# A two-layer decoder trunk on one core: other buffers, ties and positions for the loads and modulation rows of the second MLP product, and its last four steps bank by bank

## The chip, the cores and the metric

The kernel runs on 1 core of one Trainium2 chip. The metric is device time in microseconds (us) for one execution of the whole program. The engines are PE (TensorE, matrix products), DVE (VectorE), ACT (ScalarE), POOL (GpSimd) and SP (SyncE, which here only issues transfers). Each engine works through its own list of instructions in order; semaphores hold an instruction back until what it needs is there.

## What is computed

A trunk of two layers over x of 1024 tokens by 1024 channels, all in float32. Layer 0 has an S5 mixer, layer 1 a Mamba-2 mixer, and behind each mixer stands the same MLP:

```
def _sq_relu_mlp(h, w1, w2):
    a = jax.nn.relu(h @ w1)
    return (a * a) @ w2
...
    for i in range(DEPTH):                                   # DEPTH = 2
        mod = cond @ ada_w[i] + ada_b[i]
        sh1, sc1, g1, sh2, sc2, g2 = jnp.split(mod[:, None, :], N_MOD, axis=-1)
        h = _modulate(_rmsnorm(x, norm_mix_g[i]), sh1, sc1)
...
        x = x + g1 * y
        h = _modulate(_rmsnorm(x, norm_mlp_g[i]), sh2, sc2)
        x = x + g2 * _sq_relu_mlp(h, mlp_w1[i], mlp_w2[i])
    return _rmsnorm(x, final_norm_g)
```

The hidden width is 4096. `mod` is a row vector worked out from the condition c; `ada_w` is 1024 by 6144 for each layer.

## The kernel before

A float32 product is made of three matmuls: both factors are split into a high and a low part (`split`, L82 to L85: ACT makes the high part with a CAST, DVE subtracts it for the low part), and `mm3` (L113) issues high by high, high by low and low by high (L117, L118, L119).

Each MLP has two halves. `Up` (L462) makes the hidden activations in 16 pairs (`pair`, L541); it works in the PSUM banks named px and pv, reads its weights through the ring of four buffers `K.raw` (tile name raw), and writes the panels that the second half needs to DRAM. `mlp_down` (L583) makes the second product. Both use a scheme with 7 block products in place of 8. In `mlp_down` the products are q = 0 to 6, each of 8 steps s, 56 steps in all. A step has 24 matmuls of 128 by 128 by 512: two panels, four banks, three matmuls each.

A step goes through three stages. `load(n + 3)` issues its transfers three steps ahead on SP: for q = 0 the weights into two "held" tiles of 256 KB each (`raw_w`, L603), which stay for the products 1 to 3, for q > 0 the weights into `K.raw` (L608), and in each step the panel of 512 KB (`raw_b`, L613 to L615, tile name br) into one of four buffers. `prepare(n + 2)` splits the weights into whi and wlo and the panel into four tiles h01h, h01l to h71h, h71l. These are four steps deep: h01 and h11 serve the steps s = 0 and 4, h21 and h31 the steps 1 and 5, h41 and h51 the steps 2 and 6, h61 and h71 the steps 3 and 7. Then come the matmuls, and behind the last step of a product `evacuate` (L665) adds the four banks to x on DVE.

The held tiles are the other half of the same store: h00h to h70h hold the weights of the steps 0 to 3 of the first product (two each), h00l to h70l those of the steps 4 to 7.

Three other kinds of work are woven into the steps. The x tiles come back from DRAM on POOL, each behind a small ACT copy that ties the transfer to the step (L696). In layer 0, `extra()` does one of 48 modulation rows of the next layer: a transfer of 512 KB (L332) into one of two buffers and a DVE product of 1.22 us (L333). And `norm_steps` (L200) makes the norm that follows, one token half while q = 5 and 6 run, the other at the end: squares (L209), their sums over the tiles (L210), eight short matmuls (L215), an inverse square root in a dozen short DVE instructions (L217, L137 to L143), its spread over the partitions (L156).

A scheduler sets the final order on each engine out of the order in which the code asks, so an instruction can stand well ahead of where its step is written. In layer 0 the second product runs from 781 to 1104 us of the profiled execution, in layer 1 from 2195 to 2513 us.

Of the kernel before, what the change touches and what calls it, by code (L numbers as in the profile page):

```python
# [11 lines left out]
F32 = mybir.dt.float32  # L12
# [7 lines left out]
P = 128  # L20
# [3 lines left out]
KT = D // P  # L24
# [32 lines left out]
def blk(i, n=P):  # L57
    return slice(i * n, i * n + n)
# [19 lines left out]
def tmp(K, name):  # L78
    return K.tmp.tile([P, 512], F32, tag="t", bufs=6, name=name)
# [33 lines left out]
def mm3(K, ps, terms, start=True, stop=True, more=False):  # L113

    n = len(terms)
    for i, (wh, wl, xh, xl) in enumerate(terms):
        K.nc.tensor.matmul(ps, wh, xh, start=start and i == 0, stop=False, skip_group_check=more)  # L117
        K.nc.tensor.matmul(ps, wh, xl, start=False, stop=False, skip_group_check=more)  # L118
        K.nc.tensor.matmul(ps, wl, xh, start=False, stop=stop and i == n - 1, skip_group_check=more)  # L119
# [11 lines left out]
def rsqrt(K, y, v):  # L131

    V = K.nc.vector
    n = v.shape[1]
    i = K.tmp.tile([P, n], I32, tag="rsi", name="rsi")
    t = K.tmp.tile([P, n], F32, tag="rst", name="rst")
    V.tensor_scalar(i, v.bitcast(I32), 1, None, op0=ALU.logical_shift_right)  # L137
    V.tensor_scalar(i, i, -1, 0x5F3759DF, op0=ALU.mult, op1=ALU.add)
    yy = i.bitcast(F32)
    for _ in range(3):  # L140
        V.scalar_tensor_tensor(t, yy, -0.5, yy, op0=ALU.mult, op1=ALU.mult)
        V.tensor_tensor(t, t, v, op=ALU.mult)
        V.scalar_tensor_tensor(y, t, 1.5, yy, op0=ALU.add, op1=ALU.mult)  # L143
        yy = y
# [55 lines left out]
def norm_steps(K, x, half, each, bank, order):  # L200

    nc = K.nc
    ss = K.br.tile([P, HT], F32, tag="ss", name="ss", bufs=1)
    for n, k in enumerate(order):
        if n == 0:
            nc.scalar.activation(ss, x[k][half], AF.Square)
        else:
            sq = tmp(K, "sq")
            nc.scalar.activation(sq, x[k][half], AF.Square)  # L209
            nc.vector.tensor_tensor(ss, ss, sq, op=ALU.add)  # L210
        yield
    yield
    pt = bank(K)
    for j in range(4):
        nc.tensor.matmul(pt[:, j:j + 1], ss[:, blk(j)], K.ones, start=True, stop=True)  # L215
    v = K.tmp.tile([P, 4], F32, tag="rsv", name="rsv")
    nc.vector.tensor_scalar(v, pt[:, 0:4], 1.0 / D, EPS, op0=ALU.mult, op1=ALU.add)  # L217
    y = K.tmp.tile([P, 4], F32, tag="rsy", name="rsy")
    rsqrt(K, y, v)
    for _ in range(4):  # L220
        yield
    pb = spread(K, y, bank)
    for k in range(KT):
        each(k, pb)
        yield

# [50 lines left out]
def drain(gen):  # L277
    for _ in gen:
        pass
# [182 lines left out]
class Up:  # L462
# [9 lines left out]
    def bank(self, m):  # L472
        K = self.K
        return (K.ps if m % 4 < 2 else K.psb).tile([P, 512], F32, tag="ps", name="px")
# [108 lines left out]
def mlp_down(K, pool, x, bscr, w2, gate, xscr, mid, extra):  # L583

    nc, V = K.nc, K.nc.vector
    held = [h_tile(K, p % 8, 0, p // 8, F32) for p in range(16)]
    A11, A12, A21, A22 = range(4)

    def block(s, a, i):

        return w2[s, i, :, a * 256:a * 256 + 256].rearrange("i p c -> p i c")

    def raw_w(q, s):
        if q == 0:  # L600
            for j in range(2):
                d = held[2 * s + j].rearrange("p (i c) -> p i c", i=2)
                nc.sync.dma_start(d, block(s, A11, slice(2 * j, 2 * j + 2)))  # L603
            return None
        raws = []
        for a in ((A21,), (A22,), (A12,), (A21, A22), (A22,), (A12,))[q - 1]:
            t = K.raw.tile([P, 1024], F32, tag="raw", name="raw")
            nc.sync.dma_start(t.rearrange("p (i c) -> p i c", i=4), block(s, a, slice(0, 4)))  # L608
            raws.append(t)
        return raws  # L610

    def raw_b(q, s):
        t = (K.wz, pool)[s // 2 % 2].tile([P, 1024], F32, tag="br", name="br", bufs=2)  # L613
        t = t.rearrange("p (a t) -> p a t", a=2)
        nc.sync.dma_start(t, bscr[q][s].rearrange("a p t -> p a t"))  # L615
        return t

    def split_w(q, s, raw):
        wt = K.wring[(K.wturn + 1) % len(K.wring)]
        hd = held[2 * s:2 * s + 2]  # L620
        if q == 4:
            V.tensor_tensor(raw[0], raw[0], raw[1], op=ALU.add)  # L622
        if q > 2:
            return unit_of(K, raw[0])
        K.wturn = (K.wturn + 1) % len(K.wring)
        hi = wt.tile([P, 1024], F32R, tag="whi", name="whi")
        lo = wt.tile([P, 1024], F32R, tag="wlo", name="wlo")
        for j in range(2):
            c = half_of(j)
            if q == 1:  # L630
                V.tensor_tensor(hd[j], hd[j], raw[0][:, c], op=ALU.subtract)
            elif q == 2:
                V.tensor_tensor(hd[j], raw[0][:, c], hd[j], op=ALU.subtract)
            split(K, hi[:, c], lo[:, c], hd[j])
        return hi, lo

    def split_w3(s, raw):
        for j in range(2):
            c = half_of(j)
            V.tensor_tensor(raw[:, c], raw[:, c], held[2 * s + j], op=ALU.subtract)  # L640

    def split_b(s, t):
        b = []
        for j in range(2):
            k = (2 * s + j) % 8
            b.append((h_tile(K, k, 1, 0), h_tile(K, k, 1, 1)))
            split(K, *b[j], t[:, j])
        return b

    steps = [(q, s) for q in range(7) for s in range(8)]  # L650
    raws, ready = {}, {}

    def load(n):
        if n < len(steps):
            raws[n] = raw_w(*steps[n]), raw_b(*steps[n])

    def prepare(n):
        if n < len(steps):
            q, s = steps[n]
            w, b = raws.pop(n)  # L660
            if q == 3:
                split_w3(s, w[0])
            ready[n] = split_w(q, s, w), split_b(s, b)

    def evacuate(q, i, p):  # L665
        def add(m, f):
            V.scalar_tensor_tensor(x[m][f], p, gate[:, m:m + 1], x[m][f], op0=ALU.mult, op1=ALU.add)  # L667

        a, b = 2 * i, 2 * i + 1
        for m, f in (  # L670
            ((a, 1),), ((b, 0), (b, 1)), ((b, 1),), ((a, 0),), ((b, 0), (a, 0)), ((b, 1),), ((a, 1),)
        )[q]:
            add(m, f)

    def banks(q):
        if q in (0, 6):
            return [(K.ps if i < 2 else K.psb).tile([P, HT], F32, tag="ps", name="py") for i in range(4)]
        if q in (1, 3, 5):
            return [psw(K) if i < 3 else pss(K) for i in range(4)]

    for n in range(3):
        load(n)
    prepare(0)
    prepare(1)
    norms = iter(())
    X = None
    back = [(k, 1) for k in range(0, KT, 2)] + [(k, f) for k in range(1, KT, 2) for f in range(2)]
    back += [(k, 0) for k in range(0, KT, 2)]
    for n, (q, s) in enumerate(steps):
        load(n + 3)  # L690
        prepare(n + 2)
        (wh, wl), b = ready.pop(n)
        if 0 < n <= len(back):

            k, f = back[n - 1]
            nc.scalar.copy(x[k][f][:, 0:1], b[0][0][:, 0:1].bitcast(F32))  # L696
            nc.gpsimd.dma_start(x[k][f], xscr[k, :, half_of(f)])
        if s == 0:
            X = X if q == 4 or q == 2 else banks(q)
            if q == 0:  # L700
                first = X
            if q in (2, 4):
                X = first
        for j in range(2):
            for i in range(4):
                c = blk(2 * i + j)
                mm3(
                    K, X[i], [(wh[:, c], wl[:, c], *b[j])],
                    q not in (2, 4) and s == 0 and j == 0, s == 7 and j == 1, more=True,
                )  # L710
        if s == 7:
            for i in range(4):
                evacuate(q, i, X[i])
        if q == 4 and s == 7:
            norms = mid(0, lambda K: K.ps.tile([P, 512], F32, tag="ps", name="pn"), range(KT))
        elif q == 5 or q == 6 and s < 3:
            next(norms, None)
            next(norms, None)
        elif q == 6:
            if s == 3:  # L720
                drain(norms)
                norms = mid(1, pss, [1, 3, 5, 7, 0, 2, 4, 6])
            if s < 7:
                next(norms)
        extra()
    drain(norms)


# [1053 lines left out]
```

## Time and profile before

| | |
|---|---|
| median of 3 runs | 2531.93 us (2530.64 to 2536.54) |
| profiled execution, its own time | 2533.94 us |
| its span, first to last instruction | 2532.2 us |
| PE busy | 2451.7 us (97%) |
| DVE busy | 1914.6 us (76%) |
| ACT busy | 1167.9 us (46%) |
| mean granted clock of TensorE | 0.986 of full speed |

The span is 1.74 us shorter than the execution's own time. PE is busy nearly always, so that what can be won lies in the few places where it waits, and in what its clock does behind them: the granted clock has two levels, 2.4 GHz (1.00 in the rows) and 1.2 GHz (0.50), and a stretch with a value between has parts at either.

### The profile page before, as it was taken

The numbers are of one execution on the slowest core, as the hardware profiler recorded it, in microseconds if no ns is written. First come the engines' busy times: TensorE is split into PE (matmuls) and PEld (weight loads), VectorE is DVE, ScalarE is ACT, GpSimd is POOL, SyncE is SP. The second block draws the span as 40 slices with busy tenths as digits, with TensorE's granted clock in tenths as the row PEclk, the third lists the DMA queues.
The fourth block names the chain that finished last, engine by engine and source line by source line (L and its number), as shares of the span: only waits on it lengthen the run. The fifth ranks groups of instructions, "written<-read, shape, count | busy, mean of one in ns | idle before, by whom it ended". The sixth has DMA issues, their size and how long they took to land.

```text
span 2532.2 us, 32780 instructions
## 1 busy us (share of the span) xinstructions
PE 2451.7 (97%) x11624; PEld 1965.7 (78%) x11624; DVE 1914.6 (76%) x3265; ACT 1167.9 (46%) x1955; POOL 213.7 (8%) x400
## 2 busy tenths in 40 slices
PE   7999999999998999999999999999999999899997
PEld 2788788877776888777888878778888777688886
DVE  8798754967887997958596868789687777776664
ACT  4587412744444433534564655544255444444342
POOL 0010000112221000100000000000011222200000
PEclk9999999999999999999999999999999999999998
DMA  6576772467769979723455554584245666874752
GB/s 243 155 169 169 242 242 96 153 204 250 258 227 343 342 260 308 272 85 115 154 160 160 161 173 139 169 259 136 88 141 192 225 231 232 294 250 136 254 194 77
DMA packets 284645, 503.80 MB, mean 199 GB/s; under 512 B 22081, under 2 KB 162369, under 8 KB 284481
## 3 DMA queue, kind: packets, MB, share of 16 engines
q1 hardware_dynamic: 242496, 386.34, 47.3%
q0 software_dynamic: 32384, 106.98, 12.4%
q10 hardware_dynamic: 9600, 8.39, 1.0%
q8 instruction: 91, 1.49, 0.2%
q14 instruction: 74, 0.60, 0.1%
HBM read 364.27 MB, written 133.17 MB: 196 GB/s over the span
## 4 chain that ended last, share of the span: by engine, by line
PE 74%; issue 8%; DVE 6%; DMA 6%; ACT 4%; POOL 2%; SPq 0%; DVEq 0%; POOLq 0%; ACTq 0%
PE pd L118 10%; PE pd L117 10%; PE pd L119 10%; PE py L117 4%; PE py L118 4%; PE py L119 4%; PE px L117 3%; PE pm L117 2%; PE pm L118 2%; PE pm L119 2%; PE px L119 2%; PE px L118 2%; PE pv L117 2%; PE pv L118 2%; PE pv L119 2%
## 5 line engine op out<-in xcount | busy, mean ns | idle before, releaser
L84 ACT CAST whi<-raw 128x1024 fp32r<-128x1024 f32 x241 | 251.0, 1048 | 365.5 <-PE pd L118 146.3
L85 DVE TENSOR_TENSOR wlo<-raw,whi 128x1024 fp32r<-128x1024 f32 x241 | 293.2, 1218 | 113.6 <-ACT whi L84 110.2
L333 DVE SCALAR_TENSOR_TENSOR ada<-ada,cond 128x1024 f32<-128x1024 f32 x88 | 107.3, 1222 | 57.8 <-DMA ada<-in_ada 57.7
L498 ACT ACTIVATE s<-s 128x512 f32<-128x512 f32 x84 | 53.0, 631 | 158.5 <-DVE s L496 155.9
L390 POOL DMA_DIRECT2D hscr<-x x32 | 17.3, 541 | 953.6 <-DVE x L736 751.1
L1235 DVE SCALAR_TENSOR_TENSOR cacc<-cr,conv,cacc 128x1024 f32<-128x1024 f32 x72 | 91.7, 1279 | 0.9 <-ACT cacc L1216 0.8
L1288 ACT ACTIVATE L<-csb,cs 128x128 f32<-128x128 f32 x224 | 69.9, 391 | 38.4 <-DMA csb<-csr 33.7
L505 POOL DMA_DIRECT2D b<-s x96 | 51.8, 540 | 330.9 <-ACT s L499 281.7
L496 DVE TENSOR_TENSOR s<-s,px 128x512 f32<-128x512 f32 x60 | 41.0, 684 | 34.9 <-PE px L119 34.9
L496 DVE TENSOR_TENSOR s<-s,pv 128x512 f32<-128x512 f32 x36 | 24.7, 686 | 55.5 <-PE pv L119 55.5
L505 POOL DMA_DIRECT2D b<-tt x96 | 51.8, 540 | 43.0 <-DVE tt L510 25.8
L499 ACT ACTIVATE s<-s 128x512 f32<-128x512 f32 x84 | 53.2, 633 | 2.7
L1239 ACT ACTIVATE cth<-cacc 128x512 f32<-128x512 f32 x48 | 27.7, 625 | 41.4 <-DVE cacc L1235 41.3
L667 DVE SCALAR_TENSOR_TENSOR x<-py,mod,x 128x512 f32<-128x512 f32 x40 | 27.3, 744 | 25.6 <-PE py L119 25.6
L1215 ACT COPY cr<-pd 128x512 f32<-128x512 f32 x48 | 27.8, 579 | 35.0 <-PE pd L119 35.0
L1308 DVE SCALAR_TENSOR_TENSOR y<-xs,cst,pm 128x128 f32<-128x128 f32 x128 | 38.3, 342 | 4.8 <-PE pm L1305 4.8
L117 PE MATMUL pd<-h00h,whi 128*128 128x512 f32 (+1 forms) x97 | 39.7, 411 | 2.0 <-ACT h00h L237 1.8
L1106 ACT ACTIVATE gt<-pd,bgh 128x512 f32<-128x512 f32 x16 | 11.0, 685 | 65.5 <-PE pd L119 65.5
L117 PE MATMUL pd<-h01h,whi 128*128 128x512 f32 x97 | 39.4, 407 | 0.5 <-DVE h61h L736 0.5
L119 PE MATMUL pd<-h10h,wlo 128*128 128x512 f32 (+1 forms) x97 | 39.3, 405 | 0.0
L622 DVE TENSOR_TENSOR raw<-raw 128x1024 f32<-128x1024 f32 x16 | 19.6, 1225 | 26.0 <-DMA raw<-in_w 26.0
L118 PE MATMUL pd<-h00l,whi 128*128 128x512 f32 (+1 forms) x97 | 38.8, 400 | 0.4 <-DVE h00l L238 0.4
(996 smaller groups left out, 8173.0 us busy)
## 6 DMA issues: line engine op xcount, KB each, us to landing
raw<-in_w SPq DMA_DIRECT2D x204, 512.0 KB, 4.6
br<-b SPq DMA_DIRECT2D x112, 512.0 KB, 4.7
ada<-in_ada SPq DMA_DIRECT2D x96, 512.0 KB, 5.0
b<-s POOLq DMA_DIRECT2D x96, 256.0 KB, 2.9
b<-tt POOLq DMA_DIRECT2D x96, 256.0 KB, 3.8
csb<-csr SPq DMA_DIRECT2D x32, 512.0 KB, 4.5
raw<-in_w_xbc SPq DMA_DIRECT2D x24, 512.0 KB, 4.5
xscr<-cacc SPq DMA_DIRECT2D x24, 512.0 KB, 2.7
```

What stands on the lines that cost most here:

```text
L84: K.nc.scalar.copy(hi, src)
L85: K.nc.vector.tensor_tensor(lo, src, hi.bitcast(F32), op=ALU.subtract)
L117: K.nc.tensor.matmul(ps, wh, xh, start=start and i == 0, stop=False, skip_group_check=more)
L118: K.nc.tensor.matmul(ps, wh, xl, start=False, stop=False, skip_group_check=more)
L119: K.nc.tensor.matmul(ps, wl, xh, start=False, stop=stop and i == n - 1, skip_group_check=more)
L333: K.nc.vector.scalar_tensor_tensor(r, r, 1.0, K.cond, op0=ALU.mult, op1=ALU.mult, accum_out=acc)
L496: nc.vector.tensor_tensor(t, t, p, op=ALU.add)
L498: nc.scalar.activation(t, t, AF.Relu)
L499: nc.scalar.activation(t, t, AF.Square)
L505: self.K.nc.gpsimd.dma_start(self.bscr[DOWN.index(nm)][m // 2][m % 2], t)
L1235: V.scalar_tensor_tensor(acc, cr[:, t:t + L], K.cw[:, i, t:t + 1], acc, op0=ALU.mult, op1=ALU.add)
L1288: nc.scalar.activation(Lm[:, r, :], cb[:, r, :], AF.Relu, bias=S.cs[:, c0 + r:c0 + r + 1], scale=-1.0)
```

## The change

Four things are changed, all in `mlp_down` and in the generator `norm_steps`.

1. The panels of the first product (q = 0) go through the ring `K.raw` in place of the four br buffers.
2. `load` gets a token, a column of the step's own first panel tile. For q = 0 and s of 3 or more, an ACT copy of that one column into the held tile (128x1) stands ahead of the held tile's transfer, which so waits for the step: ten copies for each layer. `load` also comes behind `ready.pop`.
3. The modulation rows: two for each step in q = 0, one in q = 1 to 3, none in q = 4 and 5, one in the steps 0 to 3 of q = 6, the rest behind them. `norm_steps` yields once more, and the tiles of its last loop follow `order`.
4. The last four steps of q = 6 are taken bank by bank: all four steps of one bank (24 matmuls), its evacuation, a step of the last norm, then the next bank. This holds for both layers.

```diff
     pb = spread(K, y, bank)
-    for k in range(KT):
+    yield
+    for k in order:
         each(k, pb)
...
-    def raw_w(q, s):
+    def raw_w(q, s, after):
         if q == 0:
             for j in range(2):
+                if after is not None:
+                    nc.scalar.copy(held[2 * s + j][:, 0:1], after)
                 d = held[2 * s + j].rearrange("p (i c) -> p i c", i=2)
                 nc.sync.dma_start(d, block(s, A11, slice(2 * j, 2 * j + 2)))
...
     def raw_b(q, s):
-        t = (K.wz, pool)[s // 2 % 2].tile([P, 1024], F32, tag="br", name="br", bufs=2)
+        if q == 0:
+            t = K.raw.tile([P, 1024], F32, tag="raw", name="br")
+        else:
+            t = (K.wz, pool)[s // 2 % 2].tile([P, 1024], F32, tag="br", name="br", bufs=2)
...
-    def load(n):
+    def load(n, after=None):
         if n < len(steps):
-            raws[n] = raw_w(*steps[n]), raw_b(*steps[n])
+            raws[n] = raw_w(*steps[n], after), raw_b(*steps[n])
...
     for n, (q, s) in enumerate(steps):
-        load(n + 3)
+        if q == 6 and s == 4:
+            break
+        (wh, wl), b = ready.pop(n)
+
+        token = b[0][0][:, 0:1].bitcast(F32)
+        load(n + 3, token)
         prepare(n + 2)
-        (wh, wl), b = ready.pop(n)
...
-        elif q == 5 or q == 6 and s < 3:
+        elif q == 5 or q == 6:
             next(norms, None)
             next(norms, None)
...
-        extra()
+        if q == 0:
+            extra()
+        if q not in (4, 5):
+            extra()
+
+    drain(norms)
+    norms = mid(1, pss, [1, 3, 5, 7, 0, 2, 4, 6])
+    load(n + 3)
+    prepare(n + 2)
+    prepare(n + 3)
+    for i in range(4):
+        next(norms)
+    last = [ready.pop(n + s) for s in range(4)]
+    for i in range(4):
+        for s, ((wh, wl), b) in enumerate(last):
+            for j in range(2):
+                c = blk(2 * i + j)
+                mm3(K, X[i], [(wh[:, c], wl[:, c], *b[j])], False, s == 3 and j == 1, more=True)
+        evacuate(6, i, X[i])
+        next(norms)
     drain(norms)
```

What this does to the order of the instructions shows at three places.

SP, where the second product of layer 0 begins, before the change. b_84 to b_91 are the panels of the steps 0 to 7 of q = 0, b_92 and up those of q = 1; raw is a weight of q = 1, ada a modulation row. The sixteen held tiles and the panel b_84 stand ahead of these rows:

```order
L603 DMA h60l<-in_w 128x2x256
L603 DMA h70l<-in_w 128x2x256
L608 DMA raw<-in_w 128x4x256
L615 DMA br<-b_85 128x2x512
L615 DMA br<-b_88 128x2x512
L608 DMA raw<-in_w 128x4x256 x3
L615 DMA br<-b_89 128x2x512
L615 DMA br<-b_92 128x2x512
L615 DMA br<-b_86 128x2x512
L615 DMA br<-b_87 128x2x512
L332 DMA ada<-in_ada 128x1024 x2
L615 DMA br<-b_90 128x2x512
```

The same place with the change, from its beginning:

```order
L621 DMA br<-b_84 128x2x512
L621 DMA br<-b_85 128x2x512
L621 DMA br<-b_86 128x2x512
L621 DMA br<-b_87 128x2x512
L621 DMA br<-b_92 128x2x512
L606 DMA h00h<-in_w 128x2x256
L606 DMA h10h<-in_w 128x2x256
L606 DMA h20h<-in_w 128x2x256
L606 DMA h30h<-in_w 128x2x256
L606 DMA h40h<-in_w 128x2x256
L606 DMA h50h<-in_w 128x2x256
L606 DMA h60h<-in_w 128x2x256
```

The panels of the steps 2 and 3 (b_86, b_87) stand ahead of all held tiles, where before they stood behind them, four raws and five other panels; h00l, which stood ahead of h00h, now stands behind h70h, and the raws of q = 1, four of which stood ahead of b_84, behind all panels of q = 0.

ACT, same layer, behind the cast of the last held tile of step 2, before the change. x copies tie the return of x, s and r are of `Up`:

```order
L487 COPY s_6455<-px 128x512
L487 COPY s_6470<-pv 128x512
L84 CAST h01h<-br 128x512
L84 CAST h11h<-br 128x512
L84 CAST whi<-h00l 128x512
L84 CAST whi<-h10l 128x512
L84 CAST h21h<-br 128x512
L84 CAST h31h<-br 128x512
L573 ACTIVATE r<-px 128x512
L84 CAST whi<-h60h 128x512
```

With the change, from the cast of h21h on (ahead of it stand the same two copies, the casts of h01h and h11h, and the ties of h60h and h70h):

```order
L84 CAST h21h<-br 128x512
L604 COPY h00l<-h21h 128x1
L84 CAST h31h<-br 128x512
L604 COPY h10l<-h21h 128x1
L705 COPY x_6537<-h21h 128x1
L84 CAST whi<-h00l 128x512
L84 CAST h41h<-br 128x512
L84 CAST whi<-h10l 128x512
L84 CAST h51h<-br 128x512
L84 CAST h61h<-br 128x512
L574 ACTIVATE r<-px 128x512
L84 CAST whi<-h60h 128x512
```

The casts of the steps 2 and 3 (h41h, h51h, h61h) have moved up, ahead of r, and r now stands behind the casts of h00l and h10l, whose transfers are tied to h21h a few rows above.

DVE at the end of the kernel, before the change (the four evacuations, the four sums of squares, the start of the inverse square root):

```order
L667 SCALAR_TENSOR_TENSOR x_18804<-py,mod,x_18804 128x512
L667 SCALAR_TENSOR_TENSOR x_18808<-py,mod,x_18808 128x512
L667 SCALAR_TENSOR_TENSOR x_18812<-py,mod,x_18812 128x512
L667 SCALAR_TENSOR_TENSOR x_18816<-py,mod,x_18816 128x512
L210 TENSOR_TENSOR ss<-ss,sq 128x512 x4
L217 TENSOR_SCALAR rsv<-pn 128x4
```

With the change:

```order
L673 SCALAR_TENSOR_TENSOR x_18814<-py,mod,x_18814 128x512
L210 TENSOR_TENSOR ss<-ss,sq 128x512
L673 SCALAR_TENSOR_TENSOR x_18818<-py,mod,x_18818 128x512
L210 TENSOR_TENSOR ss<-ss,sq 128x512
L673 SCALAR_TENSOR_TENSOR x_18822<-py,mod,x_18822 128x512
L210 TENSOR_TENSOR ss<-ss,sq 128x512
L673 SCALAR_TENSOR_TENSOR x_18826<-py,mod,x_18826 128x512
L210 TENSOR_TENSOR ss<-ss,sq 128x512
L217 TENSOR_SCALAR rsv<-pn 128x4
```

Each sum now follows its own evacuation, so that one sum stands behind the last evacuation where four stood.

The modulation rows on DVE in layer 0, counted up to the split of a step's panel, before and with the change: 6 and 6 at step 8, 9 and 13 at step 11, 15 and 18 at step 14, 16 and 19 at step 15, 20 and 23 at step 18, 34 and 36 at step 31. Between the steps 36 and 42 (q = 4, s = 4 to q = 5, s = 2) stand 8 rows before and 3 with the change; the last four stand at the same place in both, right ahead of the inverse square root of the first norm half.

## Rows read from the trace of the kernel before

**Rows 1.** Waits of PE over the whole kernel: total us, times, longest us

```profile
PE py L117 <- ACT h41h L84: 10.7, 2, 5.9
PE px L117 <- ACT s L487: 6.1, 2, 3.1
```

**Rows 2.** 20-us stretches: PE, PEld, DVE, ACT, POOL busy (instructions), granted clock, DMA share, GB/s

```profile
760.00:780.00 20.00, 16.98 (x67) 13.47 (x66) 14.79 (x25) 8.03 (x14) 1.80 (x4) 0.91 0.97 328
780.00:800.00 20.00, 15.19 (x61) 11.88 (x60) 15.73 (x27) 9.76 (x22) 5.96 (x11) 0.91 1.03 373
800.00:820.00 20.00, 20.00 (x82) 16.26 (x81) 16.86 (x29) 7.67 (x16) 1.64 (x3) 0.92 0.90 323
820.00:840.00 20.00, 20.00 (x89) 16.49 (x89) 19.38 (x34) 9.36 (x20) 2.18 (x4) 1.00 0.99 348
1040.00:1060.00 20.00, 17.00 (x72) 13.74 (x71) 17.35 (x36) 8.04 (x12) 1.03 (x2) 0.91 0.78 264
...
2200.00:2220.00 20.00, 14.07 (x54) 10.91 (x53) 11.15 (x19) 6.99 (x15) 2.19 (x4) 0.83 1.01 355
```

**Rows 3.** ACT's timeline, second product's start: start, length, instruction, [idle before, releaser]

```profile
770.57 0.58 ACT L487 COPY s<-px 128x512 f32<-128x512 f32 x1
...
781.35 0.60 ACT L573 ACTIVATE r<-px 128x512 f32<-128x512 f32 x1 [0.61 <-PE px L119]
...
796.50 0.62 ACT L84 CAST h41h<-br 128x512 fp32r<-128x512 f32 x1 [0.23 <-DMA br<-b]
```

**Rows 4.** SP's timeline, same place: issues (the x4 are b_89, b_92, b_86, b_87)

```profile
775.02 3.96 SPq L615 DMA_DIRECT2D br<-b  x2
783.61 6.66 SPq L615 DMA_DIRECT2D br<-b  x4
```

**Rows 5.** PE's timeline, the fourth bank's first matmul in step 0, layer 0

```profile
783.25 0.39 PE L117 MATMUL py<-h01h,whi 128*128 128x512 f32 x1
```

**Rows 6.** DVE's and PE's timeline around the first norm half, layer 0

```profile
1009.62 1.23 DVE L333 SCALAR_TENSOR_TENSOR ada<-ada,cond 128x1024 f32<-128x1024 f32 x1 [3.03 <-DMA ada<-in_ada]
1041.63 1.22 DVE L333 SCALAR_TENSOR_TENSOR ada<-ada,cond 128x1024 f32<-128x1024 f32 x1 [1.46 <-DMA ada<-in_ada]
1047.16 0.15 DVE L217 TENSOR_SCALAR rsv<-pn 128x4 f32<-128x4 f32 x1
...
1051.53 1.35 PE L156 MATMUL pn<-ident,rsy 128*128 128x128 f32 x8 [3.00 <-DVE rsy L143]
```

**Rows 7.** The end of the kernel, DVE, ACT and PE

```profile
2510.97 2.84 DVE L667 SCALAR_TENSOR_TENSOR x<-py,mod,x 128x512 f32<-128x512 f32 x4 [18.61 <-PE py L119]
2511.81 2.66 ACT L209 ACTIVATE sq<-x 128x512 f32<-128x512 f32 x4 [20.18 <-DVE x L667]
2513.72 3.07 DVE L210 TENSOR_TENSOR ss<-ss,sq 128x512 f32<-128x512 f32 x4
2516.85 1.87 PE L215 MATMUL pn<-ones,ss 128*128 128x1 f32 x8 [3.83 <-DVE ss L210]
```

**Rows 8.** Panel splits on DVE and the matmuls that need them, steps 12 and 44

```profile
838.19 0.68 DVE L85 TENSOR_TENSOR h01l<-br,h01h 128x512 fp32r<-128x512 f32 x1
...
855.07 0.39 PE L117 MATMUL pm<-h01h,whi 128*128 128x512 f32 x1
...
1027.77 0.69 DVE L85 TENSOR_TENSOR h01l<-br,h01h 128x512 fp32r<-128x512 f32 x1
...
1030.88 0.40 PE L117 MATMUL pm<-h01h,whi 128*128 128x512 f32 x1
```

**Rows 9.** Modulation rows on DVE: the first, the 16th and the 19th of 48

```profile
800.55 1.22 DVE L333 SCALAR_TENSOR_TENSOR ada<-ada,cond 128x1024 f32<-128x1024 f32 x1
...
853.33 1.22 DVE L333 SCALAR_TENSOR_TENSOR ada<-ada,cond 128x1024 f32<-128x1024 f32 x1 [0.92 <-DMA ada<-in_ada]
...
865.64 1.23 DVE L333 SCALAR_TENSOR_TENSOR ada<-ada,cond 128x1024 f32<-128x1024 f32 x1 [0.48 <-DMA ada<-in_ada]
```

**Rows 10.** Everything on tile ada, 780 to 880 us: its last line

```profile
DMA to landing us min/median/max: 4.3/5.8/8.7
```

More of the change, by code (lines that the diff above doesn't have):

```diff
@@ L689, in mlp_down @@
     for n, (q, s) in enumerate(steps):
-        load(n + 3)
+        if q == 6 and s == 4:
[3 more added lines that the diff above has]
+        load(n + 3, token)
         prepare(n + 2)
-        (wh, wl), b = ready.pop(n)
         if 0 < n <= len(back):
             k, f = back[n - 1]
-            nc.scalar.copy(x[k][f][:, 0:1], b[0][0][:, 0:1].bitcast(F32))
+            nc.scalar.copy(x[k][f][:, 0:1], token)
             nc.gpsimd.dma_start(x[k][f], xscr[k, :, half_of(f)])
@@ L715, in mlp_down @@
             norms = mid(0, lambda K: K.ps.tile([P, 512], F32, tag="ps", name="pn"), range(KT))
-        elif q == 5 or q == 6 and s < 3:
+        elif q == 5 or q == 6:
             next(norms, None)
             next(norms, None)
[L719 to L724, printed above, removed]
-        extra()
+        if q == 0:
[17 more added lines that the diff above has]
+        next(norms)
     drain(norms)
```

## The prediction

> **What bounds the kernel now.** I read the waits of PE over the whole kernel first. PE is busy 97% of the span, so only its waits and the halved clock behind them are to be won. Two entries come once in each layer and lie where the change works: PE waits for the cast of h41h (10.7 us, 2 times) and for a copy of s (6.1 us, 2 times) [rows 1].
>
> The 20-us stretches price these waits, clock included: at full clock PE does 89 matmuls in a stretch, 0.2247 us each. Layer 0 has 61 and 82 in the two stretches behind the h41h wait, 28 and 7 short; layer 1 has 54, 35 short in one. So this wait costs 35 x 0.2247 = 7.9 us in each layer, more than its length because the granted clock of these stretches falls to 0.91 and 0.83. The stretch of the s copy has 67, 22 short: 4.9 us [rows 2]. The one in layer 1 waits as long [rows 1].
>
> ACT's timeline and SP's issues then give the cause. h41h belongs to step 2. Its cast runs at 796.50 and had waited for its panel [rows 3]; that panel (b_86) is the third of four panels that SP issued from 783.61 to 790.3, behind two earlier panels [rows 4]. The transfers ahead of it ran at 0.97 and 1.03 of the 16 DMA engines [rows 2]. So the panel of step 2 comes late by its place in SP's list. The s copy stands at 770.57 on ACT [rows 3], in order behind six casts of held tiles.
>
> A third wait is in layer 0 alone: the spread of the first norm half stands 3.00 us for the inverse square root, whose first instruction, rsv at 1047.16, comes behind modulation rows that waited for their transfers [rows 6]. That stretch has 72 matmuls; 8 of them are the short ones of the spread, 25 slots minus 0.7 us of their own is 4.9 us [rows 2]. At the end of the kernel the four sums take 3.07 us behind the last evacuation, and PE stands 3.83 us [rows 7].
>
> **The change part by part.**
>
> *Panels of q = 0 through the ring, and held tiles tied.* Now b_84 to b_87 take the four ring buffers that the first raws of q = 1 had, and are issued where those were, ahead of all held tiles. The cover for the casts of the steps 0 to 3 is then Up's own last pairs. What could be late next is a held tile of step 3 or later. Its tie is the cast of a panel three steps ahead of its use, 3 x 5.5 = 16.5 us (the steps 12 to 44 take (1030.88 - 855.07) / 32 = 5.5 us each [rows 8]), against at most 8.7 us from issue to landing in the rows that I have [rows 10], and about 2.5 us of casts and subtractions. That fits. So the h41h waits go: **-15.7 us** for both layers.
>
> *One transfer fewer ahead of the s copy.* h00l stood ahead of h00h on SP; now it stands behind. 256 KB (0.262 MB) at the stretch's 328 GB/s is 0.8 us [rows 2]. The casts ahead of the s copy are the same. The bounds are 0 and the whole 4.9 us for each layer; I take one transfer, **-1.5 us** for both.
>
> *ACT's ties and r.* A 128x1 copy costs ACT 0.2 us or less beside a 0.62-us cast, and ACT is not what is waited for: nothing for the ten copies themselves. But r, which frees the bank that the fourth group of step 0 needs, now stands behind the casts of h00l and h10l, whose transfers start only after the cast of h21h. Before, r ran from 781.35 to 781.95 and the group began at 783.25, so there is 1.3 us of room [rows 3, 5], 0.5 us with PE 0.8 us earlier. h21h can be cast when PE has left that tile, which is nine matmuls behind the end of the s copy at 771.15, some of them at half clock: about 775. With 3 to 5 us for the first transfer (the shortest landing of one of twice the size is 4.3 us [rows 10]), 0.8 us for the second, and 0.5 us for each of four casts behind it and r's own 0.6, r ends between 781.4 and 783.8 or so. I take 0.5 us late in each layer: **+1 us**, bounds 0 and 3 us for each plus a clock drop (below).
>
> *More modulation rows early.* In layer 0 DVE's lead falls while PE works through the steps: the first low tile of step 12 is ready at 838.87 and needed at 855.07, 16.2 us ahead; that of step 44 at 1028.46 for 1030.88, 2.4 us [rows 8]. Now PE comes 8.7 us sooner (7.9 + 0.8) and three more rows stand ahead of step 15. A row is 1.14 to 1.22 us of DVE; but its two buffers pace it too. The first 16 rows came every (853.33 - 800.55) / 15 = 3.52 us [rows 9]. With a first row at 797 (800.55 before [rows 9]; in the order it follows step 5's split, which no longer waits for step 2, and I take 3.5 us off) the 19th stands at 797 + 18 x 3.52 = 860.4, and with what follows it in step 15 (two low tiles of 0.6 us, a wlo of 1.2, and its own 1.2) step 15 is ready 3.7 us later: 864.1. PE wants step 15 at 780.4 + 15 x 5.5 = 862.9 (step 0 began nine matmuls ahead of 783.25 [rows 5], and 0.8 us come off). So DVE is just late there: I take **+2 us**. Bounds: 0, as q = 0 has fewer transfers beside the rows, and 11.6 us at the 4.10 us that the 16th to the 19th row took [rows 9].
>
> *No rows in q = 4.* Between the steps 36 and 42 five rows go, 5 x 1.2 = 6 us of DVE, and with them the waits for transfers of which one was 3.03 us [rows 6]. The last four rows stay right ahead of rsv. Against that PE comes up to 8.7 us sooner, less what it loses above. The lead at q = 5 should grow by some 6 + 4 + 2 - 8.7 = 3 us, as much as the wait was. I take 70% of the 4.9 us: **-3.5 us**; bounds 0 and 4.9.
>
> *Last steps bank by bank.* One sum instead of four stands behind the last evacuation. The last square ends at 2514.47 (2511.81 + 2.66) and one sum of 0.77 us follows: 2515.2 in place of 2516.79 [rows 7], **-1.5 us**. The first bank now wants the operands of step 55 three quarters through its 5.5 us, 4.1 us after its start, where three whole steps lay ahead of them before: some 12 us earlier. The tiles are four steps deep and nothing but splits is left for DVE and ACT there, so I cost nothing; bounds 0 and 3 us, since in layer 0 the lead was 2.4 us at step 44 [rows 8]. In layer 0 the evacuations come odd tiles first and the next mixer starts with an even one: nothing, bounds -0.5 and +1.2.
>
> Sum: -15.7 - 1.5 + 1 + 2 - 3.5 - 1.5 = -19.2 us. The profiled execution took 2533.94 us, so 2514.7; the median of the runs shown lies 2.0 us below it, so **2513 us**.
>
> **A rule against the change.** In q = 0 and 1 the transfers beside PE are near the top: the stretches show 348 GB/s at a DMA share of 0.99, and 373 at 1.03 [rows 2]. A step of q = 1 with two modulation rows moves four times 0.524 MB and an x tile of 0.262 MB, 2.36 MB; at 348 GB/s that is 6.8 us against 5.5 us of PE. Eight such steps would lose 10 us. The lead of 16 us absorbs this, less the 8.7 us by which PE comes sooner: 3 us late. The Trainium skill, "DMA: Bandwidth & Descriptors" (Bandwidth), puts what a core gets from HBM at about 358 GB/s; by that a step would take 6.6 us, and the loss would be 9 us. The trace agrees in most stretches and is above it in one, 373 GB/s.
>
> **The rivals.**
>
> A. *r becomes the wait*, in both layers. For it: the casts in front of r now hang on transfers issued 6 us ahead of need. Against: the queue is nearly empty then, since the ties hold it back. 1.3 us of wait and half a 3.4-us stretch at half clock (the s copy's 4.9 us for 3.0 of wait shows 1.9 lost by the clock) is 3 us a layer instead of 0.5: 2518.
>
> B. *DVE and the transfers fall behind in q = 1 and 2 of layer 0.* For it: the row pace of 4.10 us and the sum of MB above. Against: fewer rows later give it back. 6 to 11.6 us instead of 2: 2517 to 2523, with the q = 5 wait back 2526.
>
> C. *Slower*: the modulation rows' two buffers pace DVE. At the longest landing of 8.7 us [rows 10] and 1.22 us of work a pair of rows takes 9.9 us, 4.96 each; the 19th row at 886, step 15 at 890, 27 us late: 2513 + 25 = 2538. It ends above no change from 2532 on, at 4.7 us a row. Against: no stretch of the rows was that slow.
>
> D. *The wait only moves*, to step 3, 4 or 7, whose held tiles now wait for their ties: 2 x 7.9 less is won, some 2529.
>
> E. *All of it goes*: the s copy and q = 5 waits too, as with only six held tiles unhindered SP stands still and the rest of the transfers get through sooner: 9.8 - 1.5 + 1.4 + 3 = 12.7 us more, half of it likely: 2500 to 2507.
>
> **How the numbers follow.** My sum (2509 to 2517) 0.50; A 0.14; B 0.18; E 0.08; D 0.05; C 0.05. About 0.2% (5.1 us) is what a measurement of this kernel can tell from no change; faster means under 2526.9. Sum, A, B and E are faster, 0.90, less a little of B: 0.88; D and that little 0.07; C 0.05. The range reaches over E and B, 2503 to 2526, and leaves out C, D and the ends of E.
>
> **What would show it.** Right: no wait for h41h at the first product in either layer, 89 matmuls in the stretches there; the s waits 0.8 us shorter; the sum of squares ending 2.2 us after the last matmul. Wrong: PE waiting in step 0 for r (A), waits of py or pm on whi, wlo or low tiles in the steps 12 to 20 of layer 0 (B, C), on h60h or later held tiles (D), or still on rsy in q = 5. What would make the number wrong first is the pace of the rows in q = 1.

## The result

The changed kernel takes 2515.98 us in the median of 4 runs (2514.26 to 2518.23), the kernel before 2531.78 us (2530.64 to 2536.54, 4 runs): ratio 0.9937 with a 95% interval of 0.992 to 0.9953. The same kernel compared once more (last experiment below) gave 0.993 (0.9916 to 0.9944). The prediction had 2513 us. The profiled execution took 2515.34 us with a span of 2513.6 us, 18.6 us less than before.

The waits of PE in the second product of layer 0, in the changed kernel (total us, times, longest us):

```profile
PE py L119 <- DVE wlo L85: 2.8, 1, 2.8
PE pm L119 <- DVE wlo L85: 2.2, 1, 2.2
PE px L117 <- ACT s L488: 2.0, 1, 2.0
PE pn L156 <- DVE rsy L143: 0.5, 1, 0.5
PE py L118 <- DVE h01l L85: 0.5, 1, 0.5
```

The wait for h41h [rows 1] has no row any more, in either layer. The s wait is 2.0 us where it was 3.0 ([rows 1] has both layers together). New are two waits for wlo, the low parts of the weights, which DVE makes. The 20-us stretches say where (PE, PEld, DVE, ACT, POOL busy, granted clock, DMA share, GB/s):

```profile
780.00:800.00 20.00, 20.00 (x89) 16.50 (x88) 11.33 (x20) 7.13 (x15) 3.62 (x7) 1.00 1.06 389
800.00:820.00 20.00, 20.00 (x90) 16.40 (x89) 18.13 (x31) 8.43 (x18) 1.64 (x3) 1.00 0.95 328
820.00:840.00 20.00, 20.00 (x89) 16.36 (x88) 18.73 (x33) 4.89 (x11) 1.64 (x3) 1.00 0.96 342
840.00:860.00 20.00, 17.82 (x71) 14.18 (x70) 16.42 (x30) 7.91 (x16) 1.64 (x3) 0.91 0.94 314
860.00:880.00 20.00, 19.50 (x83) 14.88 (x82) 18.74 (x34) 6.94 (x12) 0.00 (x0) 1.00 0.98 344
880.00:900.00 20.00, 17.22 (x68) 13.58 (x67) 20.00 (x34) 7.41 (x13) 0.00 (x0) 0.91 0.83 289
...
1040.00:1060.00 20.00, 19.48 (x90) 15.87 (x89) 19.72 (x39) 9.14 (x14) 2.17 (x4) 1.00 0.79 270
```

Where [rows 2] had 61 and 82 matmuls (780 to 820 us) there are now 89 and 90. But 840 to 860 and 880 to 900 have 71 and 68, at a granted clock of 0.91. Before, these two were full:

```profile
840.00:860.00 20.00, 20.00 (x89) 16.39 (x88) 16.84 (x33) 8.34 (x18) 2.18 (x4) 1.00 0.99 351
880.00:900.00 20.00, 20.00 (x90) 16.43 (x89) 20.00 (x34) 8.48 (x15) 0.00 (x0) 1.00 0.75 243
```

The stretch of the first norm half has 90 in place of 72. One of the two new waits, on DVE and PE (start, length, instruction, [idle before, releaser]):

```profile
848.29 1.23 DVE L334 SCALAR_TENSOR_TENSOR ada<-ada,cond 128x1024 f32<-128x1024 f32 x1 [1.79 <-DMA ada<-in_ada]
...
849.53 0.68 DVE L85 TENSOR_TENSOR wlo<-h30l,whi 128x512 fp32r<-128x512 f32 x1
...
850.26 0.50 PE L119 MATMUL pm<-h21h,wlo 128*128 128x512 f32 x1 [2.18 <-DVE wlo L85]
```

PE waits for a low part, which stands on DVE behind a modulation row, which waits for its transfer.

The same events in both traces, as the time at which PE gets to them, give the account of the whole change (us from the start of the span; the step numbers are those of the prediction):

| PE starts | before | after | difference | gained (-) or lost since the row above |
|---|---|---|---|---|
| a px matmul of layer 0's first product, untouched by the change | 682.9 | 678.4 | -4.4 | -4.4 |
| layer 0, step 0 | 781.15 | 774.44 | -6.7 | -2.3 |
| step 3 | 805.54 | 791.14 | -14.4 | -7.7 |
| step 13 | 860.51 | 846.11 | -14.4 | 0 |
| step 19 | 893.45 | 889.32 | -4.1 | +10.3 |
| step 46 | 1042.93 | 1038.81 | -4.1 | 0 |
| step 48 | 1059.62 | 1051.42 | -8.2 | -4.1 |
| a px matmul of layer 1 | 2132.7 | 2125.9 | -6.8 | +1.4 |
| layer 1, step 0 | 2194.76 | 2184.78 | -10.0 | -3.2 |
| step 3 | 2219.53 | 2202.92 | -16.6 | -6.6 |
| the last py matmul | 2512.62 | 2496.15 | -16.5 | +0.1 |
| end of the span | 2532.2 | 2513.6 | -18.6 | -2.1 |

The first row is no part of the change: at that event the twelve profiles of this study (the change and its variants) stand between 4.9 us ahead of before and 1.9 us behind it, and each engine's instructions are the same up to there. The granted clock is not: up to that event it stands at 0.50 for 30.7 us before and for 17.1 us in the changed kernel (a mean of 0.98 and 0.99). So 4.4 of the 18.6 us between the two profiles come from no instruction that the change moved.

### The profile page after: what moved, and what is told of

The parts are those of the page before. It is cut to its first block, busy times and chain, and to the rows that moved or that the text cites. A ratio compares the mean times of both kernels' runs of the same rounds, so it can differ in the third digit from the quotient of the medians.

```text
span 2513.6 us, 32763 instructions
## 1 busy us (share of the span) xinstructions
PE 2443.5 (97%) x11624; PEld 1955.2 (78%) x11624; DVE 1914.0 (76%) x3265; ACT 1168.0 (46%) x1975; POOL 214.7 (9%) x400
## 4 chain that ended last, share of the span: by engine, by line
PE 68%; DVE 12%; DMA 10%; issue 5%; ACT 4%; POOL 1%; SPq 0%; DVEq 0%; POOLq 0%; ACTq 0%
PE pd L118 10%; PE pd L117 10%; PE pd L119 10%; DMA ada<-in_ada 3%; PE px L117 3%; PE py L117 3%; PE py L119 3%; PE py L118 3%; PE px L118 3%; PE px L119 3%; PE pv L117 2%; PE pv L118 2%; PE pv L119 2%; DVE ada L334 2%; DVE wlo L85 1%
## 5 line engine op out<-in xcount | busy, mean ns | idle before, releaser
L209 ACT ACTIVATE sq<-x 128x512 f32<-128x512 f32 x28 | 16.8, 625 | 55.0 <-DVE x L673 48.7
```

## The experiments

Two theories for the 10.3 us that PE loses between the steps 13 and 19. Theory R: more modulation rows stand ahead there. Theory T: the ties bring the held tiles late, so that DVE's lead never grows. DVE is idle from 783.1 to 788.2 us in the changed kernel, since the cast that it waits for (h11h) stands on ACT behind that of a held tile (h20l), which waits 7.42 us for its tied transfer:

```profile
787.06 0.62 ACT L84 CAST whi<-h20l 128x512 fp32r<-128x512 f32 x1 [7.42 <-DMA h20l<-in_w]
787.59 0.61 ACT L84 CAST h11h<-br 128x512 fp32r<-128x512 f32 x1
```

Each group of experiments ran beside the kernel before, whose median there was 2528.83 us (e1 to e4), 2530.63 us (e6 to e10) and 2532.58 us (e11 to e13). So kernels of different groups are compared by their ratios to it.

**Rows in their old positions (e1_rows_old).**

```diff
-        if q == 0:
-            extra()
-        if q not in (4, 5):
-            extra()
+        extra()
```

> The change with its modulation rows put back (one row in each of the steps up to q = 6, s = 3, the other three parts kept). In the changed kernel PE loses 10.3 us between the steps 13 and 19 of layer 0, in waits for low tiles of the weights (wlo), and wins 4.1 us at q = 5. Theory R, the rows ahead of step 15 do it (3 to 5 more of them, 1.2 us of DVE and some wait for a transfer each): the loss falls to some 4 us, the q = 5 wait comes back with 4 us, together 2514 us. Theory T, the ties do it (the held tiles come late, and DVE stands idle from 782 to 795 us): the loss stays at 9 to 10 us and the q = 5 wait comes back, 2520 us.

Measured: 2512.71 us, ratio 0.9936 (0.9925 to 0.9948, 5 runs). Waits of PE in layer 0's second product:

```profile
PE pn L156 <- DVE rsy L143: 6.0, 1, 6.0
PE px L117 <- ACT s L488: 1.8, 1, 1.8
PE py L117 <- ACT r L574: 0.6, 1, 0.6
```

The whole loss is gone, not half of it: PE keeps what it has won from step 3 to step 46. The rsy wait at q = 5 is back, longer than before (6.0 us against 3.0), and PE's lead over before falls from 9.3 us at step 46 to 5.8 at step 48. The time can't be told from the change's. So taking the early rows away is enough to end the loss, even with the ties; but it pays 7.6 of the 10.3 us back between the steps 46 and 48 (3.5 us lost there in place of 4.1 won), and what is left is too little for these runs to tell.

**No ties (e2_no_ties).**

```diff
-        load(n + 3, token)
+        load(n + 3)
```

> The change without its ties: the held tiles of q = 0 are loaded as soon as SP comes to them, and the ten ACT copies are gone; panels through the ring, rows and banks as in the change. Theory T: DVE's idle time at 782 to 795 us goes from some 9 us to 2 or 3, step 7 has 14 us of lead or more instead of 7, and the loss in the steps 13 to 19 of layer 0 falls from 10.3 us to 3 or less: 2508 to 2510 us. Theory R: the lead of step 7 grows, but the rows still eat it by step 15; the loss stays above 7 us, 2513 to 2516 us. In both the wait for r in layer 1 (1.4 us) should go.

Measured: 2510.56 us, ratio 0.9941 (0.9923 to 0.9958, 6 runs): not told from the change by its time, and short of the 2508 to 2510 us that theory T had by the ratio. The trace has the loss cut to 2.1 us (from step 18 to 19), with the first low tile of step 7 ready 12.2 us ahead of PE's first matmul on it instead of 7.2; no h41h wait, no r wait, and waits for s of 2.4 and 2.5 us:

```profile
PE px L117 <- ACT s L488: 2.4, 1, 2.4
PE py L119 <- DVE wlo L85: 1.8, 1, 1.8
PE pd L118 <- DVE h01l L239: 0.7, 1, 0.7
```

Either theory's cause taken away removes four fifths of the loss or all of it. The ties take some 5 us of DVE's lead at step 7, the rows the rest: with the new rows alone the lead still falls to 0.3 us at step 19, and the whole loss needs both. And the panels in the ring cure the h41h wait without the ties.

**Rows alone on the kernel before (e3_rows_only).**

```diff
-        extra()
+        if q == 0:
+            extra()
+        if q not in (4, 5):
+            extra()
```

> The kernel before with the new positions of the modulation rows alone. The h41h wait holds PE back there, so the lead of 13 to 16 us in the steps 8 to 20 of layer 0 takes 3 to 5 more rows without a wait, and the q = 5 wait (4.9 us with the clock) goes: 2527 to 2528 us by both theories. At 2531 us or more, the rows would win nothing by themselves, and the 4.1 us seen at q = 5 would belong to something else.

Measured: 2522.83 us, ratio 0.9979 (0.9969 to 0.9989, 11 runs), 5.3 us less. In layer 0 PE keeps its time to step 46 and gains 4.9 us from there to step 48; the rsy wait is gone. With the h41h wait still there, the rows cost nothing early on.

**Banks alone (e4_banks_only)** on the kernel before; the rest of the new loop's end as in the change, and the one more yield of `norm_steps`.

```diff
+        if q == 6 and s == 4:
+            break
...
+    last = [ready.pop(n + s) for s in range(4)]
+    for i in range(4):
+        for s, ((wh, wl), b) in enumerate(last):
...
+        evacuate(6, i, X[i])
+        next(norms)
```

> The kernel before with the last four steps of q = 6 taken bank by bank (and the extra yield of the norm), nothing else. My sum has 1.5 us for one sum instead of four behind the last evacuation; the profile of the change shows 2.1 us at the end. So 2529.5 to 2530.5 us; 2531.5 if the late operands of step 55 or the other order at the end of layer 0 give it back.

Measured: 2528.97 us, ratio 1.0003 (0.9994 to 1.0011, 11 runs). The end of the trace does what it should: one sum behind the last evacuation, PE's short matmuls 2.23 us behind it where [rows 7] had 3.83:

```profile
2513.03 0.75 DVE L670 SCALAR_TENSOR_TENSOR x<-py,mod,x 128x512 f32<-128x512 f32 x1 [3.35 <-PE py L119]
2514.48 0.69 DVE L210 TENSOR_TENSOR ss<-ss,sq 128x512 f32<-128x512 f32 x1 [0.69 <-ACT sq L209]
...
2515.22 1.05 PE L215 MATMUL pn<-ones,ss 128*128 128x1 f32 x8 [2.23 <-DVE ss L210]
```

Its profiled span is 2529.8 us, 2.4 less than before. The timed runs don't show it: the interval reaches from -1.5 to +2.8 us and just leaves out the 2 us. Every profile with the banks has this gain at its end, 1.6 to 2.4 us, and the two variants without them (e3, e6) have none; what gives it back in the timed runs of e4 isn't seen in its one profile.

**Panels through the ring alone (e6_ring_only)** on the kernel before: no ties, old rows, old end.

```diff
-        t = (K.wz, pool)[s // 2 % 2].tile([P, 1024], F32, tag="br", name="br", bufs=2)
+        if q == 0:
+            t = K.raw.tile([P, 1024], F32, tag="raw", name="br")
+        else:
+            t = (K.wz, pool)[s // 2 % 2].tile([P, 1024], F32, tag="br", name="br", bufs=2)
```

The rest of its edit (a token that no `load` is given, `ready.pop` ahead of `load`) issues no instruction.

> The kernel before with part 1 alone: the panels of q = 0 through the ring, no ties, old rows, old end. If the place of the panels on SP is the whole cause of the h41h waits, both go and 15.7 us are won in the two layers, the q = 5 wait stays or grows by a few us, as PE comes sooner there: ratio 0.994 to 0.996. If the ties are needed too (the sixteen held tiles then compete with the panels), a wait of 2 us or more for h21h, h41h or whi stands in the steps 1 to 4 of a layer. The waits for s should be some 0.5 to 1 us longer than with the ties (2.4 against 1.5 to 2.0 us).

Measured: 2514.85 us, ratio 0.9941 (0.9925 to 0.9956, 6 runs), 14.9 us less: its time can't be told from the whole change's. No wait for h41h, h21h or whi in the steps 1 to 4; 7.9 us gained from step 0 to step 3 of layer 0 and 8.3 us of layer 1. No run sets the ring's buffers apart from the place on SP that they bring. The waits for s are 2.8 and 3.2 us, so h00l's new place alone does not make them 2.0 and 1.4 us as in the change.

**Few rows early (e7_rows16).**

```diff
-        if q == 0:
-            extra()
-        if q not in (4, 5):
+        if q < 4 and s % 2 == 0:
             extra()
```

> The change with one modulation row in every second step of q = 0 to 3 and the other 32 asked for behind the second product; in the order they then stand 10 ahead of step 15 where the change has 20, 12 ahead of step 17 where it has 23, and the rest is drawn forward into q = 2 to 5. Theory R (DVE's time for the rows, added to what the ties took): the lead at step 15 rises by about 10 x 1.2 = 12 us, no PE wait for wlo in the steps 13 to 19. If a wait above 2 us stays there, the rows aren't the cause. A wait for rsy in q = 5 (as 43 of 48 rows stand ahead of rsv, 13 of them behind step 31) of 0 to 6 us.

Measured: 2523.38 us in one run. PE waits for nothing from step 3 to the start of step 29, but the lead doesn't rise to 14 us: step 15's first low tile is ready 9.1 us ahead, about as in e1 (9.2). So theory R holds as to the waits and fails as to the lead: with few rows something else keeps it at 9 us, which this run doesn't show. The price comes later, where the 32 rows are drawn forward: waits of 0.8 us for h31l in q = 3, 2.9 us for h61l in q = 4, 8.1 us for rsy, and 3.4 us for a tile of the norm in q = 6.

**Four buffers for the rows (e9_ada4, and e13_ada4_timed, the same kernel timed).**

```diff
-    pool, bufs = (K.adap, 2) if K.adap else (K.raw, 4)
+    pool, bufs = (K.adap, 4) if K.adap else (K.raw, 4)
```

> The change with four buffers for the modulation rows instead of two. More rows are drawn forward by it (14 ahead of step 9 where the change has 8, 17 against 13 ahead of step 11, 21 against 20 ahead of step 15). If the two buffers pace the rows (my prediction's 3.5 to 4.1 us a row), the loss in the steps 13 to 19 of layer 0 falls from 10.3 us to 4 or less, and DVE waits less for ada than the 9 us it does between 780 and 880. If it is DVE's time (DVE was busy for 16 to 19 of 20 us there), the loss is as large or larger and comes sooner, at the steps 8 to 12.

> The change with four buffers for the modulation rows, now timed. In its one look the loss at the steps 13 to 19 was 0.8 us instead of 10.3 and no rsy wait stood in q = 5. If that holds, it beats the change by 5 to 10 us: ratio to the kernel before 0.989 to 0.992. If its one time was chance, it is equal to the change.

Measured: 2506.34 us in one run (e9); 2505.23 us, ratio 0.9902 (0.9885 to 0.992, 5 runs) in e13, 25 us less than before and 7 us (by the ratios) to 9 us (by the medians) less than the change beside it, though the two intervals just touch. The loss is 0.8 us in both profiles, and no rsy wait stands in q = 5. DVE's longest waits from 780 to 880 us, first in the change, then with four buffers (e13):

```profile
DVE ada L334 <- DMA ada<-in_ada: 10.3, 10, 2.2
DVE h11l L85 <- ACT h11h L84: 5.1, 1, 5.1
```

```profile
DVE ada L334 <- DMA ada<-in_ada: 4.1, 2, 3.3
DVE wlo L85 <- ACT whi L84: 2.6, 3, 1.2
DVE h11l L85 <- ACT h11h L84: 1.7, 1, 1.7
```

The stretches with four buffers (e13):

```profile
800.00:820.00 20.00, 20.00 (x89) 16.38 (x88) 19.11 (x34) 3.71 (x8) 1.09 (x2) 1.00 0.99 354
820.00:840.00 20.00, 19.54 (x85) 15.67 (x84) 20.00 (x35) 7.19 (x15) 1.64 (x3) 1.00 1.05 383
840.00:860.00 20.00, 20.00 (x89) 16.45 (x89) 20.00 (x36) 9.15 (x21) 2.18 (x4) 1.00 1.06 380
860.00:880.00 20.00, 20.00 (x89) 16.46 (x88) 20.00 (x34) 8.14 (x15) 0.00 (x0) 1.00 0.95 340
880.00:900.00 20.00, 20.00 (x88) 16.37 (x87) 20.00 (x35) 9.41 (x18) 0.00 (x0) 1.00 0.93 332
```

DVE does 99.1 us of work in these 100 us, in the change 92.0 (the sums of the DVE column of either). With two buffers a row's transfer is issued only when the row two ahead of it is done, and most of what DVE then waits is missing, since it has little other slack here. With four, a transfer takes even longer (9.2 us from issue to landing in the median of 780 to 880 us, 5.5 us in the change), but it is issued sooner. More rows stand ahead than in the change (14 in place of 7 ahead of step 9), and they cost less. The shorter wait for h11l is not what counts: in e12 it is 2.8 us, and the loss is as large as in the change.

**Rows between old and new, no ties (e10_spread).**

```diff
-        load(n + 3, token)
+        load(n + 3)
...
-        if q == 0:
+        if q < 4 or q == 4 and s % 2 == 0 or q == 6:
             extra()
-        if q not in (4, 5):
+        if q == 0 and s % 2 == 0:
             extra()
```

> A version meant to beat the change: no ties, panels through the ring, banks at the end, and rows between the old and the new positions (two in every second step of q = 0, one in q = 1 to 3, one in every second step of q = 4, the rest as in the change): 17 rows ahead of step 15, 20 ahead of step 17, 43 ahead of step 43. Theory: the loss at the steps 13 to 19 (2.1 us without ties) goes, and the q = 5 wait stays away as only 5 rows stand between the steps 39 and 46: 1 to 3 us better than without ties alone, ratio to the kernel before 0.991 to 0.993. If the rows at the end of q = 4 bring the rsy wait back, 0.994 or more.

Measured: 2512.55 us, ratio 0.9929 (0.9914 to 0.9943, 6 runs). No loss from step 3 to 46; an rsy wait of 2.9 us is back. Its interval holds both cases of the expectation, and its time can't be told from the change's.

**Four buffers and no ties (e11_ada4_noties)**, both edits from above.

> Four buffers for the modulation rows and no ties. Without ties the steps 4 to 8 had 4 to 5 us more lead, the waits for r (up to 1.4 us) were gone and the waits for s 0.5 to 1 us longer. Theory of both causes: no PE wait above 1 us between the steps 2 and 46 of layer 0, no rsy wait there; equal to four buffers with ties within 2 us, ratio 0.989 to 0.992. If it is 3 us or more better than that, the ties alone still cost something that the row buffers don't cure.

Measured: 2508.45 us, ratio 0.991 (0.9893 to 0.9927, 4 runs), not told from four buffers with ties. In layer 0 nothing is lost from step 3 to 46; the waits for s are 3.0 and 2.6 us. Once the rows have four buffers, the ties neither help nor harm.

**The change again (e12_change_again).**

> The changed kernel itself again, to stand beside the next two on the same chip. If its loss in q = 1 and 2 of layer 0 is part of the kernel and no chance of one execution, this profile has PE waits for wlo or low tiles of 3 us or more between the steps 10 and 20 again; ratio to the kernel before 0.992 to 0.9955.

Measured: 2514.21 us, ratio 0.993 (0.9916 to 0.9944, 5 runs). The loss between step 13 and step 19 is 10.7 us, in waits for wlo of 3.9 (2 times) and 2.7 us and one for h01l of 1.5 us. It belongs to the kernel.

## Why the prediction was right, term by term

The sum was -19.2 us and the profiled executions differ by 18.6 us. That they agree so closely is luck. 4.4 us of the 18.6 stand in the table's first row, which is no part of the change; the medians differ by 15.8 us, and in e12 the ratio gives 17.7. And three terms missed, in both directions, as the table shows.

*Panels through the ring, -15.7 us:* right. 7.7 us came in layer 0, and 6.6 us in layer 1, where a 1.4-us wait for r stands between (8.0 together). The ring and the place in SP's list that it brings were the whole cause: e6 has them alone, and both waits go.

*One transfer fewer ahead of the s copy, -1.5 us:* right in sign, mis-sized. It gave 2.3 and 3.2 us, 5.5 in all. The waits became 2.0 and 1.4 us in place of 3.0 and 3.1, and the halved clock behind them went too: at 766.04 and 2176.38, where the waits now end, no stretch of 0.50 follows. I had named h00l's place as the cause; e6 and e2, where h00l stands behind but the tied tiles do not wait, have 2.4 to 3.2 us. In the six profiles with the ties these waits are 1.0 to 2.3 us, and none of the twelve has halved clock beside it; in the seven without, before among them, they are 2.0 to 3.2 us, and eight of fourteen have. So the larger part goes with the ties, which hold ten transfers back. Part of it also comes and goes by itself: e3, which has neither ties nor ring, gained 2.6 us here in layer 0.

*r, +1 us:* right, about its size, in layer 1 only. The cast of h10l had waited for its transfer, as said:

```profile
2186.24 0.62 ACT L84 CAST whi<-h10l 128x512 fp32r<-128x512 f32 x1 [1.85 <-DMA h10l<-in_w]
2187.80 0.59 ACT L574 ACTIVATE r<-px 128x512 f32<-128x512 f32 x1
...
2188.44 0.50 PE L117 MATMUL py<-h01h,whi 128*128 128x512 f32 x1 [1.40 <-ACT r L574]
```

*More rows early, +2 us:* this is the step that was mis-sized: 10.3 us, near its bound of 11.6 and inside rival B. In plain time DVE came nearly as forecast: the first row at 795.11 (forecast 797), the 20th at 859.24, 3.38 us a row (forecast 3.52), and step 15 ready at 862.3 (forecast 864.1). But PE began step 0 at 774.44 and not at 780.4, 4.4 us of it from the table's first row, and DVE's times move with PE's: in the six profiles with the ties the first row stands 20.7 to 22.3 us behind step 0, wherever step 0 is (773.2 to 778.8 us). Reckoned from step 0, the forecast had the first row at 16.6 us and step 15 ready at 83.7; the change has 20.7 and 87.8, and e2, without the ties, 18.2 and 82.4. PE is there 15 x 5.5 = 82.5 us behind step 0 if it waits for nothing. So the step that failed first is the one that put the ties at nothing. I had made sure that a tied tile lands before PE wants it, and not asked what stands behind it in the lists. On SP the six tied loads h20l to h70l now go out from 778.26 on, right ahead of the rows' first transfers (in e2 h20l goes out 15.3 us ahead of step 0). So the first row's transfer is issued 11.3 us behind step 0 and lands 20.7 behind it, in e2 9.3 and 17.7, and DVE waits for it:

```profile
778.26 0.37 SPq L606 DMA_DIRECT2D h20l<-in_w  x1
...
785.71 1.63 SPq L333 DMA_DIRECT2D ada<-in_ada  x2
...
795.11 1.23 DVE L334 SCALAR_TENSOR_TENSOR ada<-ada,cond 128x1024 f32<-128x1024 f32 x1 [2.15 <-DMA ada<-in_ada]
```

On ACT the cast of h20l, 5.55 us behind step 0 in all seven profiles without ties, stands 10.4 to 12.6 us behind it in layer 0 of the six with ties (12.6 here), and the cast that DVE waits for stands behind that. Without the ties the loss was 2.1 us (e2), near the 2 us that I had forecast, though at step 18.

Second, I stopped at step 15. At step 18 the eight additions that follow q = 1 stand ahead of its wlo, and PE waits 2.78 us for it:

```profile
877.94 4.04 DVE L673 SCALAR_TENSOR_TENSOR x<-pm,mod,x 128x512 f32<-128x512 f32 x6
881.89 1.40 DVE L673 SCALAR_TENSOR_TENSOR x<-pn,mod,x 128x512 f32<-128x512 f32 x2
883.21 0.68 DVE L85 TENSOR_TENSOR wlo<-h50h,whi 128x512 fp32r<-128x512 f32 x1
```

Third, I had no clock in the price: the two waits of 2.18 and 2.78 us cost 4.1 and 4.7 us (the difference to before goes from -14.4 at step 13 to -10.3 at step 14, and from -8.8 at step 18 to -4.1 at step 19). That the two buffers pace the rows was right: four take the loss away, with the ties and with more rows ahead, not fewer.

*No rows in q = 4, -3.5 us:* right, 4.1 us here and 4.9 in e3. In e1, with the rows back, the wait returned with 6.0 us.

*Banks, -1.5 us:* 2.1 us in the trace, PE's wait for the sums being 2.23 us in place of 3.83; e4 doesn't show it in the time.

*The rule against the change:* the stretch at 348 GB/s that I computed with is not a limit. Here 389 GB/s stand at 780 to 800 us, and with four buffers 383 and 380 where the loss had been, at DMA shares up to 1.06. The Trainium skill's "DMA: Bandwidth & Descriptors" (Bandwidth) has about 358 GB/s as a core's limit; as a limit for these stretches the trace disagrees. The Trainium skill's "HBM Reference" (Specifications (TRN2)) says that a core that streams alone gets well above that share, about 425 GB/s; these stretches fit that. In the change 314 GB/s were moved from 840 to 860 us, where e13 moved 380 and lost 0.8 us in all: there was room in the rate, and what held the rows was their two buffers.

*Rivals:* B came true in its mechanism (the two buffers and DVE behind in q = 1 and 2), at the price that it had; what it took was covered by the s waits (4.0 us more than forecast) and, in the profiles, by the 4.4 us ahead of the change. C and D did not come: the rows took 3.38 us each and not 4.96 (C's limit for no gain is 4.6 us a row by its own sum, not 4.7), and PE waited for no held tile's transfer. A was there with 1.4 us in one layer (0.2 and 1.0 us in e12). Of E the s waits' clock came.

What stays open: the 2 us of the banks in the timed runs, and 1.4 us that PE loses between step 48 of layer 0 and layer 1. Ten of the other eleven profiles lie between 1.7 us gained and 1.8 us lost there, so no part of the change need be behind it.

## What to carry to other kernels

When a stall is removed, the work that was hidden behind it comes due: reckon the lead of each feeding engine again, from the consumer's own start, and not with the clock times of the trace before. A prefetch of two buffers that stands in the in-order list of a nearly full engine costs that engine each late landing; two more buffers were worth 7 us here, more than any order of the rows that was tried. A tied load delays not only its own reader: here a cast behind it on ACT came 5 to 7 us later and the first row behind it on SP about 3 us. So look at what stands behind a tie in every in-order list.

## What the runs showed of the hardware

One core moved 380 to 397 GB/s over 20 us (397 at 780 to 800 us of e1), at DMA shares of 1.04 to 1.06. In the changed kernel PE's waits of 1.40, 1.45 and 2.02 us had no stretch of halved clock behind them, those of 2.18 and 2.78 us had one of 3.41 us each; but in e12 a wait of 3.61 us at 851.85 had none:

```profile
840.00:860.00 20.00, 16.39 (x72) 13.18 (x71) 16.70 (x30) 7.04 (x14) 1.64 (x3) 1.00 0.88 307
```

By the steps, the 3.61 us cost 3.9, the 2.18 us cost 4.1 and the 2.78 us cost 4.7. So the price of a wait of this size is about its length, or 1.9 us more, and which of the two it is, its length doesn't tell. The first 683 us, in which no edit moved an instruction, differ by up to 6.8 us between profiles, more than a third of the change, with 17.1 to 30.7 us of halved clock in them; a sum of terms from one trace has to be read against that.
